# One decoder layer: low parts of the input projection's weights from VectorE to GpSimd, and the values' weights split whole, without precedence

## The chip, the cores and the metric

The kernel runs on one core of one Trainium2 chip. The core has a matrix engine (TensorE, in the profile PE, its weight loads PEld), a vector engine (VectorE, DVE), a scalar engine (ScalarE, ACT), a general one (GpSimd, POOL) and a queue that issues most transfers (SyncE, SP). They have programs of their own and wait for one another by semaphores. The metric is the device time of one execution in microseconds, as the median of three runs.

## The reference

One layer of a hybrid decoder in float32, for 1 x 1024 tokens of 1024 features: a norm, one combined input projection, two mixers on its columns (a gated delta rule with 4 heads of 128, a dilated attention with 8 heads of 64), one output projection, and a gated MLP of 2816 features with a short convolution. Cut to what the change touches:

```python
def hybrid_layer(x, norm1_w, w_in, conv_qkv_w, ...):
    h = rmsnorm(x, norm1_w)
    proj = h @ w_in
    qkv_a, z_a, b_a, a_a, qkv_b = (proj[..., :o1], proj[..., o1:o2], proj[..., o2:o3],
                                   proj[..., o3:o4], proj[..., o4:])
    qkv_a = silu(causal_dwconv(qkv_a, conv_qkv_w))
    qa, ka, va = ...                       # 4 heads of 128 each
    o_a = gated_delta_rule(l2norm(qa) * GDN_HEAD_DIM ** -0.5, l2norm(ka), va, g, beta)
    o_a = rmsnorm(o_a, gdn_norm_w) * silu(z)
    o_b = dilated_attention(qb, kb, vb)    # qb, kb, vb from qkv_b
    x = x + concat(o_a, o_b) @ w_out
    ...                                    # gated MLP, final norm
```

## The kernel before

**Products.** The matrix engine multiplies operands of a shortened float32 format. To keep the precision of float32, each operand is split in a high part (a copy rounded to that format) and a low part (the operand less its high part), and `mm3` makes three products of them: high by high, high by low, low by high. A product is 512 columns wide; the operands' tiles have 128 x 1024 elements.

**Splitting weights.** A raw weight tile `wst` comes by a transfer on SP's queue (`raw_weight`, two buffers). `weight` then writes the high part `whi` on ScalarE (a copy) and the low part `wlo` on VectorE (a subtraction of two tiles in SBUF), two buffers each. With `urgent` it does so in two halves of 512 columns, through `ua` and `uv`, which are ScalarE and VectorE with precedence. `split` is the same without halves and precedence; the operand `x` and others are split by it. So a `wst` buffer is free for the next transfer when both copy and subtraction have read it, and a `whi` or `wlo` buffer when TensorE has made the last product with it.

**Where it happens.** `dense` runs the input projection over a list of columns: the keys' last head, then the values of the dilated attention by token (two groups `V`, eight weight tiles in all, 24 products a tile), then twenty tiles of 48 products each: `q` and `v` of the delta rule's four heads, eight tiles of the attention's queries and keys (`a`), and the four gates `z`. `take` hands out the tile that was prepared, prepares the next one (index `i`), and starts the raw transfer of the one after it. Index 0 is the keys' tile, 1 to 8 are the values', 9 to 28 the twenty others.

`values_by_token` makes four banks of PSUM in a group, over four weight tiles. ScalarE evicts them to `vx`, scaled by the norm `rst`; the second group writes the same four banks and so waits for these evictions.

**What runs beside it.** While the values are projected, the keys' heads are prepared: a convolution of four taps on VectorE (`kT<-xr,gcw,kT`, `xr` being the input), exponentials of the decays on ScalarE (`dec`), transposed keys (`ktok` evictions, sums of squares `sq`), and evictions of the keys' products on VectorE (`um`). Later come the same for queries (`qT`) and values (`vT`), norms on GpSimd (`rq`, a power), a forward substitution in 31 steps on VectorE, clearing of tiles for it on GpSimd (`x`), and then the delta rule's chain and the attention, whose GpSimd work is the copies `rd` and the products `vtok<-vtok,ms`.

**What sets the order.** On TensorE the order is that in which a planner (`Weave`) records the products: `mm` and `tp` stamp each one (L193, L197). On all other engines a scheduler orders the instructions by a priority, which follows the order of recording, and by when it reckons their inputs to be there; instructions made through `ua` and `uv` are put 400 places ahead (L144 in the profile, others L142). GpSimd and VectorE instructions execute in the order fixed thereby.

Of the kernel before, what the change touches and what calls it, by code (L numbers as in the profile page):

```python
# [7 lines left out]
F32 = mybir.dt.float32  # L8
F32R = mybir.dt.float32r
AF = mybir.ActivationFunctionType  # L10
OP = mybir.AluOpType
# [136 lines left out]
def hybrid_layer(tc, I, out):  # L148
    nc = tc.nc
    wv = Weave()  # L150
    ve = Engine(wv, nc.vector, "vector", 0.07, 0.00105)
    ac = Engine(wv, nc.scalar, "scalar", 0.12, 0.00085)

    uv = Engine(wv, nc.vector, "vector", 0.07, 0.00105, first=tc.high_priority)
    ua = Engine(wv, nc.scalar, "scalar", 0.12, 0.00085, first=tc.high_priority)
    po_ = Engine(wv, nc.gpsimd, "gpsimd", 0.15, 0.0021)
# [10 lines left out]
    def tile_(pool, shape, dt, name, tag, bufs):  # L167
        return wv.slot(pool.tile(list(shape), dt, name=name, tag=tag, bufs=bufs), tag, bufs)
# [3 lines left out]
    def A(name, tag, dt=F32, shape=(P, 1024)):  # L172
        if tag in TURNS:
            i = turns[tag] = turns.get(tag, -1) + 1
            tag = TURNS[tag][i % len(TURNS[tag])]
        return tile_(lp, shape, dt, name, tag, SLOTS[tag])
# [23 lines left out]
    def mm3(dst, lhs, rhs, first, last, **kw):  # L200
        us = 0.2135 * rhs[0].shape[-1] / 512
        mm(dst, lhs[0], rhs[0], us, first, False, **kw)
        mm(dst, lhs[0], rhs[1], us, False, False, **kw)
        mm(dst, lhs[1], rhs[0], us, False, last, **kw)

    def split(src, hi, lo):
        ac.activation(hi, src, AF.Copy)
        return ve.tensor_tensor(lo, src, hi.bitcast(F32), op=OP.subtract)

    def raw_weight(src, n=1024):  # L210
        st = tile_(wp, [P, n], F32, "wst", "wst", 2)
        sy.dma_start(st, src)
        return st

    def weight(src, n=1024, st=None, urgent=False):
        if st is None:
            st = raw_weight(src, n)
        hi = tile_(wp, [P, n], F32R, "whi", "whi", 2)
        lo = tile_(wp, [P, n], F32R, "wlo", "wlo", 2)
        for sl in (half(0), half(1)) if urgent else (slice(0, n),):  # L220
            (ua if urgent else ac).activation(hi[:, sl], st[:, sl], AF.Copy)
            (uv if urgent else ve).tensor_tensor(lo[:, sl], st[:, sl], hi[:, sl].bitcast(F32), op=OP.subtract)
        return hi, lo

    def wk_by_halves(src):
# [34 lines left out]
    def bank(tag, name="ps"):  # L260
        return tile_(pp_, (P, 512), F32, name, tag, 2)
# [7 lines left out]
    def half(i):  # L269
        return slice(i * 512, i * 512 + 512)  # L270
# [170 lines left out]
    def scaled(pair, name, by_class=False, tag="ev", t=None, hs=(0, 1)):  # L441
        if t is None:
            t = A(name, tag)
        for h in hs:
            sl = half(h)
            if by_class:
                ve.tensor_tensor(t[:, sl].rearrange("p (n c u) -> p n u c", n=4, c=4),
                                        pair[h].rearrange("p (n u c) -> p n u c", n=4, c=4),
                                        rstdB[:, sl].rearrange("p (n u c) -> p n u c", n=4, c=4), op=OP.mult)
            else:  # L450
                ve.tensor_tensor(t[:, sl], pair[h], rstdB[:, sl], op=OP.mult)
        return t
# [4 lines left out]
    def conv_silu(xr, j, name, tag):  # L457
        y = A(name, tag)
        ac.activation(y, xr, AF.Copy, scale=gcw[:, j, 3:4])
        for d in (1, 2, 3):  # L460
            inst = ve.scalar_tensor_tensor(y[:, d:], xr[:, :S - d], gcw[:, j, 3 - d:4 - d], y[:, d:],
                                           op0=OP.mult, op1=OP.add)
            if j // 4 == 1 and d == 2 and klast:
                after(inst, klast[-1], "the keys before go first")
        if j // 4 != 1:
            ac.activation(y, y, AF.Silu)
            return y

        th = ac.activation(xr, y, AF.Tanh, scale=0.5)
        klast.append(ve.scalar_tensor_tensor(y, xr, 1.0, y, op0=OP.add, op1=OP.mult))  # L470
        kends[j - 4] = th, klast[-1]
        return y

    def silu2(xr, name):
        y = A(name, "ev")
        ac.activation(y, xr, AF.Tanh, scale=0.5)
        ve.scalar_tensor_tensor(y, y, 1.0, xr, op0=OP.add, op1=OP.mult)
        return y
# [8 lines left out]
    def first_keys():  # L487
        xr = [scaled(pst[2 * h:2 * h + 2], "xr", tag=("ev", "ev", "qa")[h]) for h in range(3)]
        for h in range(3):
            T["k", h] = conv_silu(xr[h], 4 + h, "kT", "kT*")  # L490
            wv.add(3, kprep(h))
            yield wv.need(T["k", h])

    def dense():

        yield from wv.until("first")
        yield from wv.until("norms")
        wv.add(2, first_keys())

        srcs, tiles = [], 0  # L500
        for col in DENSE:
            if col[0] == "V":
                srcs += [I["wv"][j] for j in range(4)]
            else:
                srcs.append(I["wi"][tiles])
                tiles += 1
        place = [0]
        raw = [raw_weight(srcs[0])]
        nxt = [weight(None, st=raw.pop())]
        raw.append(raw_weight(srcs[1]))  # L510

        def take():
            w = nxt.pop()
            i = place[0] = place[0] + 1
            if i < len(srcs):
                nxt.append(weight(None, st=raw.pop(), urgent=1 <= i <= 8))
            if i + 1 < len(srcs):
                raw.append(raw_weight(srcs[i + 1]))
            return w

        def values_by_token(g):

            banks = [bank(t) for t in ("asc", "asc", "ch", "ch")]
            for j in range(4):
                w = [t.rearrange("p (k m) -> p k m", k=2) for t in take()]
                for kk in range(2):
                    k = 2 * j + kk
                    for i, pt in enumerate(banks):
                        c = 4 * g + i
                        yield wv.need(pt, *w)  # L530
                        mm3(pt, [t[:, c * P:(c + 1) * P] for t in xs[k]], [t[:, kk, :] for t in w], k == 0, k == KT - 1)
            for i in range(0, 4, 2):
                vx = A("vx", "ev", shape=(P, 2, 512))
                for e in range(2):
                    c = 4 * g + i + e
                    ac.activation(vx[:, e, :], banks[i + e], AF.Copy, scale=rst[:, c:c + 1])
                c = 4 * g + i
                sy.dma_start(vpark[c * P:(c + 2) * P].rearrange("(e p) d -> p e d", e=2), vx)
            wv.done.add(("V", g))

        for i, col in enumerate(DENSE):
            kind, h = col[:2]
            if kind == "V":
                yield from values_by_token(h)
                continue
            if kind == "z":
                yield from wv.until(("o", h))
            w = [t.rearrange("p (k m) -> p k m", k=KT) for t in take()]
            pair = []
            for hh in range(2):  # L550
                pt = bank("hf")
                yield wv.need(pt, *w)
                for k in range(KT):
                    mm3(pt, [t[:, k, :] for t in w], [t[:, half(hh)] for t in xs[k]], k == 0, k == KT - 1)
                    yield 0.0

                pair.append(pt)
                if hh == 0:
                    xr = A("aqkv" if kind == "a" else "xr", "go" if kind == "k" else "ev")
                scaled(pair, "xr", kind == "a", t=xr, hs=(hh,))  # L560
            if kind == "k":
                T["k", h] = conv_silu(xr, 4 + h, "kT", "kT*")
                wv.add(3, kprep(h))
            elif kind == "q":
                q = conv_silu(xr, h, "qT", "qa")
                wv.add(4, qprep(h, q))
            elif kind == "v":
                v = conv_silu(xr, 8 + h, "vT", "qa")
                wv.add(4, vprep(h, v))
            elif kind == "z":  # L570
                og = gated[h] = A("og", "kT*")
                sy.dma_start(og, mixer[h])
                ve.tensor_tensor(og, og, silu2(xr, "zz"), op=OP.mult)
            else:
                sy.dma_start(apark[h, col[2]], xr)
                wv.done.add(col)
        wv.done.add("dense")
# [1067 lines left out]
```

## Time and profile before

| | us |
|---|---|
| median of three runs | 1209.37 (1208.98 to 1209.37) |
| the profiled execution | 1209.18 |
| its span | 1207.4 |
| GpSimd busy | 59.1 |
| ScalarE busy | 576.2 |
| VectorE busy | 925.8 |
| TensorE busy | 1192.3 |

The profile is one execution. A row of the timeline gives the start and the duration in us, the engine, the line, the operation and its tiles (out<-in by the program's names, partitions x elements), and in brackets the engine's idle time just before it with the instruction that ended it; `x3` is a run of three alike, taken together. A row of the waits gives the engine and tile that waited, what released it, the sum, the number of times and the longest. A row of the windows gives each engine's busy time in a stretch, with TensorE's granted clock as a share of full speed. Rows of a tile give the shortest, mean and longest duration in ns and the first and last start.

### The profile page before, as it was taken

How to read it: one execution, taken by the hardware profiler on the slowest of the kernel's cores; microseconds unless marked ns; L12 is line 12 of the kernel's file. 1: busy time of each engine (PE TensorE's matmuls, PEld its weight loads, DVE VectorE, ACT ScalarE, POOL GpSimd, SP SyncE). 2: the span in 40 equal slices, each digit the busy share in tenths (PEclk: the TensorE clock that was granted, in tenths of full speed). 3: DMA queues.
4: the chain of work that ended last, by engine and by line, in shares of the span. 5: the costliest groups of instructions: out<-in, count | busy, mean ns of one | idle time of the engine just before them, and what ended most of it. 6: DMA issues, size and time to landing. Idle time of an engine off the chain costs nothing.

```text
span 1207.4 us, 18350 instructions
## 1 busy us (share of the span) xinstructions
PE 1192.3 (99%) x7068; PEld 986.6 (82%) x7068; DVE 925.8 (77%) x1470; ACT 576.2 (48%) x1134; POOL 59.1 (5%) x78
## 2 busy tenths in 40 slices
PE   9999999999999999999999999999999999999997
PEld 7887888889877778888888888888888888888886
DVE  7683975666466556768988989889898889999865
ACT  7384335356355443655545445444454454444441
POOL 0211010003211000000000000000000000000000
PEclk9999999999999999999999999999999999999999
DMA  7424343435633213544223132231322298556513
GB/s 230 111 75 125 117 120 108 157 102 167 213 118 119 89 36 100 174 136 157 71 69 105 53 105 82 75 105 53 105 65 93 89 366 311 177 163 226 162 57 140
DMA packets 85798, 154.80 MB, mean 128 GB/s; under 512 B 21168, under 2 KB 36304, under 8 KB 85712
## 3 DMA queue, kind: packets, MB, share of 16 engines
q1 hardware_dynamic: 85136, 153.12, 39.3%
q8 instruction: 55, 0.90, 0.3%
q10 hardware_dynamic: 576, 0.52, 0.1%
q14 instruction: 31, 0.25, 0.1%
HBM read 117.68 MB, written 35.93 MB: 127 GB/s over the span
## 4 chain that ended last, share of the span: by engine, by line
PE 93%; DVE 3%; ACT 2%; issue 1%; DMA 1%; SPq 0%; POOLq 0%; POOL 0%; DVEq 0%; ACTq 0%
PE ps L193 44%; PE pa L193 20%; PE dw L193 17%; PE pc L193 10%; PE ps L197 3%; DVE kT L142 1%; DMA xt<-in_xT 1%; DVE wlo L142 0%; ACT dec L142 0%; DVE xr L142 0%; DVE x1h L142 0%; PE pd L193 0%; DVE qT L142 0%; SPq L142 0%; ACT xr L142 0%
## 5 line engine op out<-in xcount | busy, mean ns | idle before, releaser
L193 PE MATMUL dw<-pr 128*128 128x512 f32 (+1 forms) x984 | 211.3, 376 | 0.0
L193 PEld LDWEIGHTS dw<-pr 128*128 128x128 f32 x984 | 176.7, 188 | 33.6
L193 PE MATMUL ps<-xhi,whi 128*128 128x512 f32 x384 | 157.3, 410 | 0.0
L193 PE MATMUL ps<-xlo,whi 128*128 128x512 f32 x384 | 150.0, 391 | 0.8 <-DVE xlo L142 0.8
L193 PE MATMUL ps<-xhi,wlo 128*128 128x512 f32 x384 | 150.2, 391 | 0.0
L193 PE MATMUL pa<-T,pair 128*128 128x512 f32 x528 | 127.0, 389 | 0.0
L193 PEld LDWEIGHTS pa<-T,pair 128*128 128x128 f32 x528 | 99.0, 188 | 20.5
L193 PEld LDWEIGHTS ps<-xhi,whi 128*128 128x128 f32 x384 | 72.2, 188 | 18.1 <-issue 4.7
L193 PEld LDWEIGHTS ps<-xhi,wlo 128*128 128x128 f32 x384 | 72.1, 188 | 15.7 <-DVE wlo L142 0.2
L193 PEld LDWEIGHTS ps<-xlo,whi 128*128 128x128 f32 x384 | 72.4, 188 | 13.4 <-DVE xlo L142 1.1
L142 ACT ACTIVATE u<-pa 128x512 f32<-128x512 f32 x44 | 26.3, 598 | 107.3 <-PE pa L193 107.3
L142 DVE SCALAR_TENSOR_TENSOR y<-xu,fcw,y 128x1023 f32<-128x1023 f32 (+1 forms) x44 | 56.4, 1281 | 22.1 <-ACT y L142 22.0
L142 ACT ACTIVATE whi<-wst 128x1024 fp32r<-128x1024 f32 (+2 forms) x33 | 33.3, 1009 | 68.0 <-PE ps L193 62.4
L193 PE MATMUL pa<-B,A 128*128 128x512 f32 x264 | 63.4, 389 | 0.0
L193 PE MATMUL pc<-T,S 128*128 128x512 f32 x264 | 63.4, 389 | 0.0
L193 PE MATMUL pa<-T,S 128*128 128x512 f32 x264 | 63.4, 389 | 0.0
L193 PE MATMUL pc<-B,pair 128*128 128x512 f32 x264 | 63.4, 389 | 0.0
L142 DVE TENSOR_TENSOR wst<-wst 128x512 f32<-128x512 f32 x88 | 60.4, 687 | 0.9
L193 PE MATMUL ps<-B,pair 128*128 128x512 f32 x252 | 60.5, 389 | 0.0
L144 ACT ACTIVATE sm<-sm,mx 128x128 f32<-128x128 f32 (+7 forms) x64 | 35.4, 556 | 50.5 <-DVE mx L144 50.5
L193 PEld LDWEIGHTS pa<-T,S 128*128 128x128 f32 x264 | 49.6, 188 | 10.3
L193 PEld LDWEIGHTS pc<-T,S 128*128 128x128 f32 x264 | 49.6, 188 | 10.3
(245 smaller groups left out, 2344.7 us busy)
## 6 DMA issues: line engine op xcount, KB each, us to landing
wst<-in_wu SPq DMA_DIRECT2D x44, 512.0 KB, 3.7
wd<-in_wd SPq DMA_DIRECT2D x44, 512.0 KB, 4.5
upark<-y SPq DMA_DIRECT2D x22, 512.0 KB, 3.7
wst<-in_wi SPq DMA_DIRECT2D x21, 512.0 KB, 3.7
r<-upark SPq DMA_DIRECT2D x11, 512.0 KB, 7.5
r<-upark SPq DMA_DIRECT2D x22, 256.0 KB, 6.8
wa<-in_wd SPq DMA_DIRECT2D x22, 256.0 KB, 3.1
wst<-in_wv SPq DMA_DIRECT2D x8, 512.0 KB, 3.7
```

The lines of the kernel that those rows point to most:

```text
L142: return getattr(eng, op)(*a, **kw)
L144: return getattr(eng, op)(*a, **kw)
L193: tc.stamp_issue_order_token(nc.tensor.matmul(dst, lhs, rhs, start=start, stop=stop, **kw).ins, TOKEN)
L197: tc.stamp_issue_order_token(nc.tensor.transpose(dst, src, ident if idt is None else idt).ins, TOKEN)
```

## The change

The halves and the precedence go out of `weight`. For indices 9 to 28 (the twenty tiles from the first query head onwards) the high part is copied by ScalarE as before, and the low part is subtracted by GpSimd (`po_`) instead of VectorE. For the values' eight tiles the split is whole, on ScalarE and VectorE, without precedence; the keys' tile stays as it was.

```diff
-    def weight(src, n=1024, st=None, urgent=False):
+    def weight(src, n=1024, st=None, spare=False):
         if st is None:
             st = raw_weight(src, n)
         hi = tile_(wp, [P, n], F32R, "whi", "whi", 2)
         lo = tile_(wp, [P, n], F32R, "wlo", "wlo", 2)
-        for sl in (half(0), half(1)) if urgent else (slice(0, n),):
-            (ua if urgent else ac).activation(hi[:, sl], st[:, sl], AF.Copy)
-            (uv if urgent else ve).tensor_tensor(lo[:, sl], st[:, sl], hi[:, sl].bitcast(F32), op=OP.subtract)
+        if spare:
+            ac.activation(hi, st, AF.Copy)
+            po_.tensor_tensor(lo, st, hi.bitcast(F32), op=OP.subtract)
+        else:
+            split(st, hi, lo)
         return hi, lo
...
             if i < len(srcs):
-                nxt.append(weight(None, st=raw.pop(), urgent=1 <= i <= 8))
+                nxt.append(weight(None, st=raw.pop(), spare=i >= 9))
```

The order of TensorE's products changes by a few places only. On the other engines it moves at these places. (The rows of the order call `TENSOR_SCALAR` what the profile's rows call `SCALAR_TENSOR_TENSOR`, an operation with two tiles and a scalar.)

ScalarE, from the middle of the first group of values to its last eviction; before:

```order
L144 ACTIVATE whi<-wst 128x512 x2
L142 ACTIVATE xr<-kT 128x1024
L142 ACTIVATE dec<-dec,ngc 128x128 x8
L142 ACTIVATE ge<-gel 128x8
L144 ACTIVATE whi<-wst 128x512 x2
```

and after that, at its evictions:

```order
L142 ACTIVATE vx<-ps,rst 128x512 x3
L142 ACTIVATE dec<-dec,ngc 128x128 x5
L144 ACTIVATE whi<-wst 128x512 x2
L142 ACTIVATE dec<-dec,ngc 128x128 x3
L142 ACTIVATE eg<-gend 128x8
L142 ACTIVATE ge<-gel 128x8
L142 ACTIVATE vx<-ps,rst 128x512
```

The same two pieces in the changed kernel, in one:

```order
L142 ACTIVATE xr<-kT 128x1024
L142 ACTIVATE whi<-wst 128x1024
L142 ACTIVATE dec<-dec,ngc 128x128 x8
L142 ACTIVATE ge<-gel 128x8
L142 ACTIVATE whi<-wst 128x1024
...
L142 ACTIVATE vx<-ps,rst 128x512 x2
L142 ACTIVATE dec<-dec,ngc 128x128 x8
L142 ACTIVATE eg<-gend 128x8
L142 ACTIVATE ge<-gel 128x8
L142 ACTIVATE vx<-ps,rst 128x512 x2
L142 ACTIVATE whi<-wst 128x1024
```

`xr` goes ahead of the copy `whi`. Two evictions `vx` instead of one stand behind the eight `dec`, and the copy of the next tile stands behind them all.

VectorE, at the fourth and fifth of the values' tiles; before:

```order
L142 TENSOR_SCALAR kT<-xr,gcw,kT 128x1021
L144 TENSOR_TENSOR wlo<-wst,whi 128x512 x2
L142 TENSOR_SCALAR ssk<-ssk 128x8
L142 RECIPROCAL bp<-ssk 128x8
L142 TENSOR_TENSOR bp<-bp,beta 128x8
L144 TENSOR_TENSOR wlo<-wst,whi 128x512
L142 TENSOR_TENSOR ke<-bp,eg 128x8
L142 TENSOR_SCALAR um<-ps,bp,dec 128x128
L144 TENSOR_TENSOR wlo<-wst,whi 128x512
L142 TENSOR_SCALAR um<-ps,bp,dec 128x128 x3
L142 TENSOR_SCALAR kT<-xr,kT 128x1024
L142 COPY gel<-dec 128x8
```

and in the changed kernel:

```order
L142 TENSOR_SCALAR kT<-xr,gcw,kT 128x1021
L142 TENSOR_TENSOR wlo<-wst,whi 128x1024
L142 TENSOR_SCALAR ssk<-ssk 128x8
L142 RECIPROCAL bp<-ssk 128x8
L142 TENSOR_TENSOR bp<-bp,beta 128x8
L142 TENSOR_TENSOR ke<-bp,eg 128x8
L142 TENSOR_SCALAR kT<-xr,kT 128x1024
L142 COPY gel<-dec 128x8
L142 TENSOR_SCALAR kT<-xr,gcw,kT 128x1022
L142 TENSOR_SCALAR um<-ps,bp,dec 128x128 x4
L142 TENSOR_TENSOR wlo<-wst,whi 128x1024
```

The fourth tile's low part keeps its place as one instruction; the fifth's moves behind the next head's convolution products and four evictions `um`.

GpSimd, from the first query head onwards; before:

```order
L142 MEMSET xi 128x1024
L142 AFFINE_SELECT xi<-xi 128x1024
L142 TENSOR_TENSOR rq<-ssq,mhalf 128x8
L142 MEMSET x_1672 128x1024
L142 MEMSET x_1686 128x1024
L142 TENSOR_TENSOR rq<-ssq,mhalf 128x8 x3
```

and in the changed kernel:

```order
L142 MEMSET xi 128x1024
L142 AFFINE_SELECT xi<-xi 128x1024
L142 TENSOR_TENSOR wlo<-wst,whi 128x1024 x4
L142 TENSOR_TENSOR rq<-ssq,mhalf 128x8
L142 TENSOR_TENSOR wlo<-wst,whi 128x1024
L142 MEMSET x_1653 128x1024
L142 MEMSET x_1667 128x1024
L142 TENSOR_TENSOR wlo<-wst,whi 128x1024
L142 TENSOR_TENSOR rq<-ssq,mhalf 128x8
```

The low parts stand between the norms `rq` and the clearing of `x`; the other fourteen follow among the later work of GpSimd.

## The prediction, made before the changed kernel had been run

> **What bounds the kernel now.** I read the page first, then the waits of TensorE, then the windows and the timeline of the two places which the waits name.
>
> ```profile
> span 1207.4 us, 18350 instructions
> PE 1192.3 (99%) x7068; PEld 986.6 (82%) x7068; DVE 925.8 (77%) x1470; ACT 576.2 (48%) x1134; POOL 59.1 (5%) x78
> PE 93%; DVE 3%; ACT 2%; issue 1%; DMA 1%; SPq 0%; POOLq 0%; POOL 0%; DVEq 0%; ACTq 0%
> ```
>
> TensorE works for 1192.3 of 1207.4 us, and it makes up 93% of the chain that ended last. So 15.1 us at most can be won from waits, and an edit that takes VectorE off work wins only where TensorE waits for VectorE. These are TensorE's waits that lie at the instructions of the change:
>
> ```profile
> PE ps L193 <- ACT vx L142: 2.1, 1, 2.1
> PE ps L193 <- DVE wlo L144: 1.1, 1, 1.1
> ```
>
> Each is one single wait. The windows say how full the stages are in which the changed instructions run (values by token in the first, then heads):
>
> ```profile
> core 0: us, PE busy (x) PEld busy (x) DVE busy (x) ACT busy (x) POOL busy (x), PEclk, DMA share, GB/s
> 40.00:100.00 60.00, 56.79 (x276) 46.54 (x274) 42.62 (x78) 40.34 (x131) 10.98 (x7) 0.97 0.38 101
> 100.00:150.00 50.00, 50.00 (x246) 42.23 (x245) 36.77 (x84) 17.43 (x42) 5.51 (x4) 1.00 0.37 112
> 200.00:250.00 50.00, 49.79 (x551) 41.41 (x551) 28.21 (x52) 20.80 (x56) 3.22 (x2) 1.00 0.38 127
> ```
>
> From 40 to 100 us TensorE lacks 3.2 us; from 100 to 150 it lacks none, and from 200 to 250 only 0.2. The first half of the change works where there is something to win, the second where there is nearly nothing. The first window has a second oddity, a clock of 0.97, and a finer cut finds its place:
>
> ```profile
> 92.00:96.00 4.00, 1.89 (x10) 1.24 (x9) 1.29 (x2) 2.83 (x9) 0.00 (x0) 1.00 0.61 100
> 96.00:99.50 3.50, 3.50 (x14) 2.81 (x12) 0.00 (x0) 1.63 (x9) 0.00 (x0) 0.51 0.77 265
> ```
>
> Directly behind the emptiest stretch (1.89 of 4 us busy) the granted clock is 0.51 for 3.5 us. At half speed these 3.5 us hold work for 3.5 x 0.51 = 1.8 us, so the clock costs 1.7 us beside the wait.
>
> **The change, part one: the eight tiles of the values.** It removes the halving and the precedence; nothing else is taken out or added. By size alone it saves: two half subtractions become one whole, and the same for the copies.
>
> ```profile
> L142 DVE TENSOR_TENSOR wlo<-wst,whi x23: 1202/1225/1425, 29.9 to 476.9; 128x1024 fp32r<-128x1024 f32 x23
> L144 DVE TENSOR_TENSOR wlo<-wst,whi x18: 679/684/694, 32.0 to 498.9; 128x512 fp32r<-128x512 f32 x18
> ```
>
> A whole low part takes 1.22 us and two halves 2 x 0.684 = 1.37, 0.15 us more. What matters is when TensorE gets them. At the fourth value tile (the first wait) it is this:
>
> ```profile
> 73.54 0.50 PE L193 MATMUL ps<-whi,xhi 128*128 128x512 f32 x1
> 75.15 0.50 PE L193 MATMUL ps<-wlo,xhi 128*128 128x512 f32 x1 [1.11 <-DVE wlo L144]
> 70.57 3.92 DVE L142 SCALAR_TENSOR_TENSOR kT<-xr,gcw,kT 128x1023 f32<-128x1023 f32 x3 [0.23 <-ACT kT L142]
> 74.41 1.29 DVE L144 TENSOR_TENSOR wlo<-wst,whi 128x512 fp32r<-128x512 f32 x2
> ```
>
> The three convolution passes fill VectorE up to 74.4 in both versions, since its order there stays. The first half was ready at 74.41 + 0.68 = 75.1, and TensorE went on at 75.15. The whole tile is ready at 74.4 + 1.22 = 75.6: this wait grows by **0.46 us**. Copying the high part whole costs nothing, because VectorE is the later of the two.
>
> The next tile loses its precedence on VectorE, and is put behind one convolution product and four evictions of `um`:
>
> ```profile
> 82.57 0.39 PE L193 MATMUL ps<-wlo,xhi 128*128 128x512 f32 x1
> 76.92 1.24 ACT L144 ACTIVATE whi<-wst 128x512 fp32r<-128x512 f32 x2
> 77.96 1.15 ACT L142 ACTIVATE xr<-kT 128x1024 f32<-128x1024 f32 x1
> 80.01 1.21 DVE L142 SCALAR_TENSOR_TENSOR kT<-xr,kT 128x1024 f32<-128x1024 f32 x1
> 82.41 1.12 DVE L142 SCALAR_TENSOR_TENSOR um<-ps,bp,dec 128x128 f32<-128x128 f32 x4
> ```
>
> ScalarE now does `xr` before `whi`, so `xr` ends at about 76.9 + 1.1 = 78.0 and the product behind it starts then, 2 us before its old place. From its start to the end of the four evictions were 83.53 - 80.01 = 3.5 us; by that the low part runs from 81.5 to 82.7. TensorE wants it at 82.57 + 0.46 = 83.0. I cost this at nothing, with 0.3 us of cover; without that cover, each tenth more is a tenth on the span.
>
> The second wait is ScalarE's. Four banks must be evicted (`vx`) before the second group of values can write them:
>
> ```profile
> 81.33 2.46 ACT L142 ACTIVATE dec<-dec,ngc 128x128 f32<-128x128 f32 x8 [2.23 <-DVE gel L142]
> 83.80 1.14 ACT L144 ACTIVATE whi<-wst 128x512 fp32r<-128x512 f32 x2
> 88.83 1.88 ACT L142 ACTIVATE vx<-ps,rst 128x512 f32<-128x512 f32 x3
> 92.00 1.19 ACT L144 ACTIVATE whi<-wst 128x512 fp32r<-128x512 f32 x2
> 94.12 0.71 ACT L142 ACTIVATE vx<-ps,rst 128x512 f32<-128x512 f32 x1
> 91.92 0.40 PE L193 MATMUL ps<-whi,xhi 128*128 128x512 f32 x1
> 94.89 0.50 PE L193 MATMUL ps<-whi,xhi 128*128 128x512 f32 x1 [2.11 <-ACT vx L142]
> ```
>
> Three evictions ran at 88.83; the fourth stood behind the eight `dec` and behind the two urgent halves of 92.00, and TensorE waited 2.1 us for its bank. In the new order two evictions run first, then `dec`, two small ones, then two evictions, and the copy of the next tile only after them. ScalarE also arrives earlier: `dec` at 81.33 had waited 2.2 us for VectorE, whose product came 2 us later than it will. So the copy at 83.80 starts as soon as TensorE has left its buffer, near 83.0, and the row behind it moves up by about 0.75 us. By durations: first two evictions 88.1 to 89.35 (1.88 / 3 = 0.63 each), eight `dec` 2.46 to 91.8, the small ones to 92.1, the last two to 93.35. TensorE comes to the third bank at 91.92 + 0.46 = 92.4 and waits there until 92.8, and the fourth bank's products start near 93.5, not 94.89: **1.4 us earlier**, with the 0.46 already paid (so -1.86 for the wait itself). Bounds: nothing if `dec` is late again, -1.65 (2.11 less 0.46) if no wait remains.
>
> The **clock**: the only stretch at half speed follows a gap of over 2 us, and the gap of 1.1 us ahead of 75.15 was followed by none. With gaps of 0.4 us left here, I take the half clock as gone: **-1.7 us**; the other bound is 0. [...]
>
> **Part two: twenty low parts go to GpSimd.** VectorE is relieved of 20 x 1.22 = 24.5 us. GpSimd has no such subtraction in this trace; the nearest row is its own two-input operation of the same size:
>
> ```profile
> 288.60 1.90 POOL L142 TENSOR_TENSOR vtok<-vtok,ms 128x1024 f32<-128x1024 f32 x1
> 289.96 0.56 DVE L142 TENSOR_SCALAR ms<-ms 128x8 f32<-128x8 f32 x1 [0.28 <-ACT osq L144]
> 312.59 0.17 DVE L142 TENSOR_SCALAR ms<-ms 128x8 f32<-128x8 f32 x1 [0.47 <-ACT osq L144]
> ```
>
> So 1.9 us a tile, 38 us on an engine that was busy 59. The two rows beside it show a cost to VectorE: a tiny operation of 0.17 us lasts 0.56 when it meets GpSimd's, and both end at 290.5. [...]
>
> ```profile
> wst<-in_wi SPq DMA_DIRECT2D x21, 512.0 KB, 3.7
> 115.62 1.06 ACT L142 ACTIVATE whi<-wst 128x1024 fp32r<-128x1024 f32 x1 [6.10 <-PE ps L193]
> 121.31 0.39 PE L193 MATMUL ps<-xhi,wlo 128*128 128x512 f32 x1
> ```
>
> For the first query tile the high part is there at 116.7 and the low part wanted at 121.3, 4.6 us of cover. For an upper bound on GpSimd I add one VectorE pass that it waits out (1.3 us, a third of the 3.92 above): 3.2 us, still covered; less than 1.9 has no row for it. Later tiles are prepared a whole tile ahead, 48 products of 50.00 / 246 = 0.2 us, near 10 us. The raw tile is released some 0.7 to 2 us later, and its successor's load on SP's queue lands in 3.7 us, inside those 10. GpSimd's own queue holds short work behind the subtractions (`rq`, `rd` copies), which is then late by up to 1.9 us; I cost that at nothing, for TensorE's full windows show no place that leans on it, and at 1.9 us each if one did. One place has no cover at all, the fourth query head:
>
> ```profile
> 215.02 1.22 DVE L142 TENSOR_TENSOR wlo<-wst,whi 128x1024 fp32r<-128x1024 f32 x1 [0.18 <-ACT whi L142]
> 216.16 1.28 DVE L142 SCALAR_TENSOR_TENSOR qT<-xr,gcw,qT 128x1023 f32<-128x1023 f32 x1
> 222.31 0.77 PE L197 MATMUL ps<-ident,qT 128*128 128x128 f32 x5 [0.21 <-ACT qT L142]
> ```
>
> There TensorE already waits 0.2 us at the end of the `qT` passes. If the pass at 216.16 has to sit out GpSimd's subtraction, it begins at 216.9 instead: +0.7; if GpSimd gives way, it begins up to 1.2 us earlier and the 0.2 us go. Between -0.2 and +0.7 I take +0.2, and the same net nothing for the other 19.
>
> **Sum:** +0.46 - 1.86 - 1.7 + 0.2 = -2.9 us. The profiled execution took 1209.18 us (its span of 1207.4 and 1.8 around it), which is 0.2 under the median of the runs, 1209.37. 1209.18 - 2.9 = **1206.3 us**.
>
> **Rivals.**
>
> First, the half clock stays or moves: the gap at the fourth tile grows from 1.1 to about 1.6 us, nearer the 2.1 which was followed by half clock. Then only 1.2 us are won: 1208.0. For it: I have just these two gaps to set the limit from. Against: 1.6 is still below 2.1. [...]
>
> Second, the wait for `vx` stays: `dec` is held up by VectorE as at 81.33, and the two evictions that are now behind all eight of them come as late as the one did. Then +0.46 and +0.2, with the clock as before: 1209.8. Against it: the product ahead of `dec` moves up by 2 us.
>
> Third, slower: GpSimd and VectorE shut each other out, and each low part costs VectorE 1.9 - 1.22 = 0.68 us more than it gave. Over 20 tiles that is 13.6 us. It decides once it reaches TensorE in more than five tiles (3.1 / 0.68 = 4.6 uses up the gain); at 10 of 20 it is +6.8 - 3.1, **1212.9 us**. For it: the `ms` pair, and the convolutions, which read two tiles each and start all through the heads. Against: VectorE is busy 28.2 of 50 us at the heads from 200 to 250, so 0.68 us have room, and TensorE's wait there is 0.2 us in total.
>
> **How the numbers follow.** The forecast gets 0.43, the first rival 0.25, the second 0.12, the third 0.20. What a measurement of this kernel can tell from no change is about 0.2%, 2.4 us: faster means under 1207.0, slower over 1211.8. The forecast varies by the 0.3 us of cover, the bounds of the wait and GpSimd's ±0.5, so 1205 to 1208: four fifths of it are faster, 0.35, the rest same. The first rival spreads from 1206.5 to 1209, 0.08 faster and 0.17 same. The second is same, 0.01 to slower. The third is slower in 0.18 and same in 0.02. Together 0.43 faster, 0.38 same, 0.19 slower. The range goes from 1204.4 (all gains at their bounds, -1.65 - 1.7 - 0.2, and one subtraction of 1.22 where VectorE's relief might reach TensorE once more) to 1211.8, leaving out most of the third rival and little below; the forecast's own range is 1205 to 1208.
>
> **What would show it.** In the waits, `vx` falls from 2.1 to under 0.6 and `wlo` rises from 1.1 to about 1.6. The windows show clock 1.00 from 72 to 103; a 0.5 behind the fourth tile speaks for the first rival. GpSimd's busy time goes to about 97 us, its `wlo` group reads near 1.9 us, and VectorE's falls by about 26. At the fourth query head the wait for `qT` lies between 0 and 0.9. The prediction is wrong if TensorE's busy time grows, if waits on `wlo` of GpSimd appear, or if VectorE's passes beside them lengthen and TensorE waits for them in the heads.

## The result, and the profile after

| | median us | lowest to highest | runs |
|---|---|---|---|
| before | 1208.70 | 1206.42 to 1210.53 | 20 |
| changed | 1206.57 | 1205.53 to 1208.53 | 20 |

The ratio is 0.9983, 95% interval 0.9977 to 0.9989: the change wins about 2.1 us, 0.17%. The profiled execution took 1205.66 us with a span of 1203.8. One correction of names: the text ahead of this section counts from the keys' tile, so that what it calls the fourth and fifth value tile are the third and fourth of the values. Tiles are counted here from the first of the values.

The page and TensorE's waits of the changed kernel (columns as before):

```profile
span 1203.8 us, 18327 instructions
PE 1190.0 (99%) x7068; PEld 984.8 (82%) x7068; DVE 917.5 (76%) x1442; ACT 575.1 (48%) x1126; POOL 108.9 (9%) x98
PE ps L197 <- DVE at L142: 1.5, 1, 1.5
PE ps L193 <- DVE wlo L142: 0.9, 1, 0.9
```

The wait on `vx` is gone and a new one stands at the top: 1.5 us on VectorE's `at` (evictions of the products of keys and queries in the delta rule's heads), in a stage where TensorE never waited. GpSimd is busy 49.8 us more. VectorE is busy only 8.3 us less, though subtractions of 24.5 us were taken off it. The windows show where time was won and lost:

```profile
40.00:100.00 60.00, 59.07 (x298) 48.92 (x297) 44.17 (x82) 42.45 (x135) 14.52 (x9) 1.00 0.38 102
100.00:150.00 50.00, 49.71 (x243) 41.41 (x242) 37.97 (x78) 14.72 (x30) 12.50 (x7) 1.00 0.38 111
150.00:200.00 50.00, 48.37 (x342) 39.85 (x341) 33.56 (x55) 22.90 (x65) 17.14 (x9) 1.00 0.46 127
92.00:96.00 4.00, 4.00 (x23) 3.30 (x23) 1.23 (x1) 3.15 (x12) 0.00 (x0) 1.00 0.59 164
96.00:99.50 3.50, 3.50 (x21) 3.03 (x20) 1.92 (x6) 2.27 (x10) 1.82 (x2) 1.00 0.64 155
```

From 40 to 100 us TensorE is busy 59.07 instead of 56.79, at clock 1.00 instead of 0.97. From 92 to 96 it is full where it had 1.89 of 4, and no half clock follows. But from 150 to 200 it now lacks 1.6 us, where it lacked nothing before:

```profile
150.00:200.00 50.00, 50.00 (x354) 41.79 (x353) 35.57 (x64) 22.27 (x64) 5.62 (x4) 1.00 0.45 127
```

ScalarE's timeline at the evictions, with TensorE's third bank, has the order that the prediction laid out, and runs 0.8 to 1.1 us sooner than reckoned there:

```profile
87.27 1.34 ACT L142 ACTIVATE vx<-ps,rst 128x512 f32<-128x512 f32 x2
88.41 2.51 ACT L142 ACTIVATE dec<-dec,ngc 128x128 f32<-128x128 f32 x8
90.95 1.32 ACT L142 ACTIVATE vx<-ps,rst 128x512 f32<-128x512 f32 x2
91.75 0.50 PE L193 MATMUL ps<-whi,xhi 128*128 128x512 f32 x1
```

All four evictions end at 92.27 instead of 94.83, and TensorE passes with hardly a stop.

GpSimd's low parts, all twenty in one row of the groups, then the one of `v1` with the step of VectorE that met it, the next step of that kind, and the wait of TensorE twelve us on (timelines of the three engines):

```profile
L142 POOL TENSOR_TENSOR wlo<-wst,whi 128x1024 fp32r<-128x1024 f32 x20 | 47.7, 2385 | 123.0 <-ACT whi L142 121.3 <-PE ps L197 1.8
141.64 2.42 POOL L142 TENSOR_TENSOR wlo<-wst,whi 128x1024 fp32r<-128x1024 f32 x1 [10.36 <-ACT whi L142]
142.26 2.04 DVE L142 TENSOR_TENSOR xi<-xi,tmp 128x220 f32<-128x220 f32 x1
144.75 0.38 DVE L142 TENSOR_TENSOR xi<-xi,tmp 128x207 f32<-128x207 f32 x1
154.05 0.66 PE L197 MATMUL ps<-ident,vT 128*128 128x128 f32 x4 [1.47 <-DVE at L142]
```

A low part takes GpSimd 2.39 us, not the 1.9 that I read from `vtok`. A step of the forward substitution lasts 2.04 us where the next one, a little smaller, takes 0.38; it ends 0.24 us after GpSimd's instruction. In the chain that ended last, the stretch from 105 to 150 us has turned from TensorE (one piece of 44 us before) to VectorE, with two more long steps in it, each beside a low part of GpSimd. TensorE's wait stands at the end of this chain:

```profile
118.84 2.49 DVE xi L142
129.07 2.51 DVE xi L142
```

```profile
99.93 44.21 PE ps L193 x211
```

(The first of these fences is the changed kernel's chain, the second that of before; start, duration, what.)

### The profile page after: what moved, and what is told of

It is laid out like the page before. It is cut to its first block, busy times and chain, and to the rows that moved or that the text cites. A ratio compares the mean times of both kernels' runs of the same rounds, so it can differ in the third digit from the quotient of the medians.

```text
span 1203.8 us, 18327 instructions
## 1 busy us (share of the span) xinstructions
PE 1190.0 (99%) x7068; PEld 984.8 (82%) x7068; DVE 917.5 (76%) x1442; ACT 575.1 (48%) x1126; POOL 108.9 (9%) x98
## 4 chain that ended last, share of the span: by engine, by line
PE 90%; DVE 6%; ACT 2%; issue 1%; DMA 1%; SPq 0%; POOLq 0%; POOL 0%; DVEq 0%; ACTq 0%
PE ps L193 40%; PE pa L193 20%; PE dw L193 17%; PE pc L193 10%; PE ps L197 2%; DVE xi L142 1%; DVE kT L142 1%; DVE tmp L142 1%; DVE xr L142 1%; DMA xt<-in_xT 1%; ACT sm L144 0%; DVE qT L142 0%; DVE vT L142 0%; SPq L142 0%; DMA mt<-mdram 0%
## 5 line engine op out<-in xcount | busy, mean ns | idle before, releaser
L142 ACT ACTIVATE whi<-wst 128x1024 fp32r<-128x1024 f32 (+2 forms) x41 | 41.9, 1021 | 76.2 <-PE ps L193 48.0
L142 POOL TENSOR_TENSOR rs<-rs,mhalf 128x2 f32<-128x2 f32 (+2 forms) x4 | 4.5, 1116 | 738.8 <-DVE rs L144 738.8
L142 POOL TENSOR_TENSOR wlo<-wst,whi 128x1024 fp32r<-128x1024 f32 x20 | 47.7, 2385 | 123.0 <-ACT whi L142 121.3
```

The source lines that it names most:

```text
L142: return getattr(eng, op)(*a, **kw)
```

## The experiments

The table has every run. Each ratio is to runs of the kernel before made beside it, of which some have the half clock and some not (below); each kernel ran 5, 11 or 20 times. The lead is how much earlier (minus) or later TensorE starts its first product with a weight tile than in the profile of before, from the matmul rows of the timelines: at the sixth value tile (100.9 us in before), at `v1` (157.1), `v3` (213.9), in the attention (384.7), and behind the input projection (498.3). The profile of before had the half clock, which makes 1.6 us of each lead. Up to 0.3 us more or less in a lead arose ahead of the value stage.

| kernel | ratio to before | 95% interval | lead at 100.9 | 157.1 | 213.9 | 384.7 | 498.3 |
|---|---|---|---|---|---|---|---|
| the change | 0.9983 | 0.9977 to 0.9989 | -4.0 | -1.2 | -1.2 | -4.4 | -3.9 |
| values only | 0.9977 | 0.9969 to 0.9986 | -3.5 | -3.5 | -3.4 | -3.4 | -3.4 |
| GpSimd only | 1.0017 | 1.0008 to 1.0026 | -1.8 | +1.6 | +1.6 | -1.6 | -1.1 |
| vx first | 0.9977 | 0.9969 to 0.9986 | -4.7 | -4.7 | -4.7 | -4.7 | -4.7 |
| before again | 0.9994 | 0.9985 to 1.0003 | -0.1 | 0.0 | 0.0 | -0.1 | -0.1 |
| GpSimd from q2 | 0.9955 | 0.9942 to 0.9967 | -3.3 | -3.3 | -3.2 | -6.3 | -5.9 |
| GpSimd for the first four | 1.0010 | 1.0001 to 1.0018 | -3.6 | -0.2 | -0.2 | -0.3 | -0.3 |
| order put back | 0.9989 | 0.9980 to 0.9997 | -4.1 | -0.8 | -0.7 | -3.9 | -3.4 |
| vx first, GpSimd from q2 | 0.9955 | 0.9941 to 0.9968 | -3.7 | -3.7 | -3.7 | -6.8 | -6.3 |
| planned only | 0.9956 | 0.9944 to 0.9969 | -3.3 | -3.3 | -3.3 | -4.9 | -4.3 |
| executed only | 0.9950 | 0.9937 to 0.9964 | -3.6 | -3.6 | -3.6 | -5.7 | -6.0 |
| first four twice | 0.9983 | 0.9975 to 0.9992 | -3.3 | +1.1 | +1.1 | -2.0 | -1.5 |
| first four in eighths | 0.9963 | 0.9949 to 0.9976 | -1.9 | -1.2 | -1.1 | -4.3 | -3.8 |

### The two halves apart, the evictions alone, and before once more

The edits named GpSimd only, vx first, and vx first with GpSimd from q2 are made to the kernel before; where they use `spare`, `weight` also gets the branch `if spare` of the change, which is not printed again. All other edits are made to the changed kernel. The run before again has no edit.

```diff
-                nxt.append(weight(None, st=raw.pop(), spare=i >= 9))
+                nxt.append(weight(None, st=raw.pop(), spare=False))
```

> Only the values' half of the change: their eight tiles are split whole without precedence, and all twenty later low parts stay on VectorE. Theory (the gain is made in the value stage, by the wait on vx and the half clock behind it; GpSimd's share adds about nothing): ratio to the kernel before 0.9975 to 0.9990, the clock 1.00 from 72 to 103 us, the wait on vx gone. Rival 1 (the gain is made by VectorE's relief): ratio 0.999 to 1.001 although the value stage looks as in the changed kernel. Rival 2 (GpSimd's share costs time): ratio below 0.997, faster than the whole change.

```diff
-                nxt.append(weight(None, st=raw.pop(), urgent=1 <= i <= 8))
+                nxt.append(weight(None, st=raw.pop(), urgent=1 <= i <= 8, spare=i >= 9))
```

> Only GpSimd's half: twenty low parts on GpSimd, the values' tiles in urgent halves as before. Theory: ratio 0.999 to 1.001, the wait on vx of 2.1 us and the half clock are still there, and VectorE's passes with two SBUF inputs that meet a low part on GpSimd last up to 2.4 us longer. Rival 1: ratio 0.9975 to 0.999, as in the whole change. Rival 2: ratio above 1.001.

```diff
-                    ac.activation(vx[:, e, :], banks[i + e], AF.Copy, scale=rst[:, c:c + 1])
+                    ua.activation(vx[:, e, :], banks[i + e], AF.Copy, scale=rst[:, c:c + 1])
```

> The kernel before with one thing changed: the evictions vx have precedence on ScalarE, so that the fourth runs ahead of the urgent halves of the next tile; everything else, the halves too, as before. Theory (the wait on vx and the clock behind it are the gain): the wait on vx falls below 1 us, no half clock follows, ratio 0.997 to 0.999. Rival (the clock falls for another reason): the wait falls but some 3.4 us at half clock remain in the value stage, ratio 0.9985 to 1.000.

> The kernel before, profiled once more. If the half clock follows from the gap of 2.1 us alone, it is there again, at the same place, for some 3.5 us. [...] Ratio 0.999 to 1.001.

The values' half wins 0.23% alone, GpSimd's loses 0.17% alone. That GpSimd's share adds nothing is not borne out by the run with GpSimd only, whose interval lies wholly above 1. The threshold set for the rival that it costs time (the values alone below 0.997) was not reached either. Multiplied, the two halves would give 0.9994; the change has 0.9983, and the intervals, taken together, are too wide to say whether the halves simply add. Giving `vx` precedence, one letter in the kernel before, wins the same 0.9977 as the values' half: moving the fourth eviction is enough, and neither whole tiles nor their lower precedence are needed for it. (In its profile the lead is larger, -4.7, by 0.8 us won at the third value tile; the section on the prediction says from what.)

The clock came out differently from what I had thought. The windows of the kernel before taken again, then of the kernel with GpSimd only, whose value stage is that of before, gap and all:

```profile
92.00:96.00 4.00, 1.91 (x7) 1.19 (x6) 1.29 (x2) 2.77 (x9) 0.00 (x0) 0.87 0.63 94
96.00:99.50 3.50, 3.50 (x16) 2.90 (x15) 0.00 (x0) 1.63 (x9) 0.00 (x0) 0.66 0.74 267
```

```profile
92.00:96.00 4.00, 1.91 (x11) 1.30 (x10) 1.29 (x2) 2.62 (x8) 0.00 (x0) 1.00 0.62 88
96.00:99.50 3.50, 3.50 (x19) 2.88 (x18) 0.00 (x0) 3.18 (x19) 0.00 (x0) 1.00 0.72 260
```

In the second kernel's window nothing is slowed. In the first, the half clock lies 1.1 us earlier than in the first profile of before (there 0.50 from 96.1 to 99.5 us), and so falls in both rows; cut to it, the row reads:

```profile
95.00:98.40 3.40, 3.40 (x11) 2.73 (x12) 0.00 (x0) 1.17 (x7) 0.00 (x0) 0.50 0.87 258
```

The same wait of 2.1 us was followed by half clock in two executions and by none in the third. So its cost is paid in some executions only. The mean granted clock that each run recorded bears this out. A half clock of 3.4 us takes 3.4 x 0.50 / 1208 = 0.0014 off that mean. The end of an execution has a slower clock too (0.64 over the last 7.4 us of before, so that the stretch at 96 us is not the only slow one there; 0.58 over the last 8.8 of the changed kernel), and the eleven profiles that have clock 1.00 from 20 to 150 us stand at 0.997 or 0.998. Of the 78 runs of before beside the experiments, 41 are at 0.996 or below and take 1209.5 us in the mean, ten are at 0.998 and take 1207.5; the others, at 0.997, can be either. Of the changed kernel's 20 runs, two are at 0.996 (1208.3 us), the others above (1206.3). Of the 22 runs of the values' half and of `vx` first, none is at 0.996. Where in those runs the half clock lay is not shown.

### Which of GpSimd's twenty, and is it the order?

```diff
-                nxt.append(weight(None, st=raw.pop(), spare=i >= 9))
+                nxt.append(weight(None, st=raw.pop(), spare=i >= 13))
```

> The changed kernel, but the first four of the twenty low parts (q0, v0, q1, v1, those that are made while VectorE runs the forward substitution) go back to VectorE; sixteen stay on GpSimd. Theory (the changed kernel loses 2.8 us on the way through these four tiles and nothing behind them): no loss at 140 to 157 us, ratio 0.9955 to 0.9975. If the 2.7 us that the changed kernel gained from 213 to 498 us come from VectorE's relief there, they stay: ratio near 0.9955. Rival (that gain is only the loss caught up): ratio 0.997 to 0.9985, as with the values' half alone.

```diff
-                nxt.append(weight(None, st=raw.pop(), spare=i >= 9))
+                nxt.append(weight(None, st=raw.pop(), spare=9 <= i <= 12))
```

> The counterpart: only the low parts of q0, v0, q1 and v1 on GpSimd, the sixteen later ones on VectorE, the values' half as in the changed kernel. Theory (these four carry the loss): the loss of some 2.8 us at 140 to 157 us is there, ratio 0.999 to 1.0005. Rival (it is caught up downstream whatever the later tiles do): ratio 0.9975 to 0.9985.

```diff
                 scaled(pair, "xr", kind == "a", t=xr, hs=(hh,))
+                if kind in "qv" and h < 2 and (kind, h) != ("v", 1):
+                    n = {"q0": (10, 15), "v0": (17, 20), "q1": (22, 28)}[kind + str(h)][hh]
+                    after(steps[n], evicted[-1], "the eviction goes first")
```

(`steps` collects the substitution's products, `evicted` the evictions `xr`.)

> The changed kernel with VectorE's order put back: dependencies on the same engine hold the forward substitution's steps 10, 15, 17, 20, 22 and 28 behind the evictions xr of q0, v0 and q1, where they stood before; all twenty low parts stay on GpSimd. If the scheduler's pulling of two or three more steps ahead of these evictions is the cause of the loss, it goes: ratio 0.9955 to 0.9975. If it is that GpSimd's low part shuts VectorE out (a step of 0.4 us lasting 2.0 to 2.5), the loss stays: ratio 0.998 to 0.999, as in the changed kernel.

With four of the twenty back on VectorE, 0.9983 becomes 0.9955; with those four alone on GpSimd it becomes 1.0010. So the four cost (0.9983 - 0.9955) x 1209 = 3.4 us, and the other sixteen win (0.9977 - 0.9955) x 1209 = 2.7 us, each to some 1.8 us by the intervals. The change's small net is a difference of two larger terms. The order is not it: with the six evictions of `q0`, `v0` and `q1` back in their old places the lead still falls from -4.1 to -0.8, and the step behind an eviction is as long as in the changed kernel, or longer (VectorE's timeline of the kernel with the order put back):

```profile
141.03 0.68 DVE L142 TENSOR_TENSOR xr<-ps,rstdB 128x512 f32<-128x512 f32 x1
141.63 2.43 DVE L142 TENSOR_TENSOR tmp<-mt,xi 128x231 f32<-128x231 f32 x1
```

### Is it the exclusion?

```diff
...
             split(st, hi, lo)
+            if twice:
+                nc.gpsimd.tensor_tensor(lo, st, hi.bitcast(F32), op=OP.subtract)
...
-                nxt.append(weight(None, st=raw.pop(), spare=i >= 9))
+                nxt.append(weight(None, st=raw.pop(), spare=i >= 13, twice=9 <= i <= 12))
```

> As the run with GpSimd from q2 onwards, but the low parts of q0, v0, q1 and v1, which VectorE subtracts there, are subtracted by GpSimd once more into the same tiles; the orders of VectorE and TensorE are the same as in that run, to the last instruction. So GpSimd's four instructions are added and nothing is taken off VectorE. If GpSimd's subtraction shuts VectorE out: three or four steps of the forward substitution last 2 to 2.5 us instead of 0.3 to 0.4, VectorE is late by 6 to 8 us, and the run takes 3 to 8 us more than that one, ratio 0.998 to 1.002. If it does not: ratio 0.9945 to 0.9965.

```diff
...
-            po_.tensor_tensor(lo, st, hi.bitcast(F32), op=OP.subtract)
+            wv.account("gpsimd", 0.15 + 0.0021 * n, [lo], [st, hi], 0.28)
+            for j in range(pieces):
+                sl = slice(j * n // pieces, (j + 1) * n // pieces)
+                nc.gpsimd.tensor_tensor(lo[:, sl], st[:, sl], hi[:, sl].bitcast(F32), op=OP.subtract)
...
-                nxt.append(weight(None, st=raw.pop(), spare=i >= 9))
+                nxt.append(weight(None, st=raw.pop(), spare=i >= 9, pieces=8 if i <= 12 else 1))
```

> The changed kernel, but GpSimd subtracts the first four low parts (q0, v0, q1, v1) in eight pieces of 128 columns; the planner books the same time as before, and the orders of TensorE, VectorE and ScalarE are those of the changed kernel to the last instruction. If GpSimd keeps VectorE out for the length of one instruction and lets it in between two, steps of the forward substitution last some 0.6 to 0.8 us instead of 2.0 to 2.5, several in a row, and part of the 2.8 us lost at 140 to 157 us comes back: ratio 0.996 to 0.998. If VectorE is kept out until all pieces are done, or pays for each the same: one step still lasts 2 us or more, ratio 0.998 to 0.9995.

Four instructions are added on an idle engine, none taken off VectorE, no order of VectorE or ScalarE changed: 0.9955 becomes 0.9983, 3.4 us, and the lead falls by 4.4 us at the same place. TensorE doesn't wait for the second writing of the low parts: the waits that are new in this kernel are for what VectorE and, behind it, ScalarE deliver.

```profile
PE ps L197 <- ACT qT L142: 1.9, 1, 1.9
PE ps L197 <- DVE at L142: 1.3, 1, 1.3
```

So the loss is that of VectorE being kept out while GpSimd's subtraction runs, called the exclusion from here on. In VectorE's timeline of the kernel that does them twice, a step takes 2.44 us, and two convolution passes 3.42 where 1.28 is usual:

```profile
122.30 2.44 DVE L142 TENSOR_TENSOR tmp<-mt,xi 128x192 f32<-128x192 f32 x1
133.61 3.42 DVE L142 SCALAR_TENSOR_TENSOR qT<-xr,gcw,qT 128x1023 f32<-128x1023 f32 x1
145.55 3.42 DVE L142 SCALAR_TENSOR_TENSOR vT<-xr,gcw,vT 128x1023 f32<-128x1023 f32 x1
```

In eighths the engines take turns. GpSimd's row and three of VectorE's of that kernel:

```profile
142.09 5.02 POOL L225 TENSOR_TENSOR wlo<-wst,whi 128x128 fp32r<-128x128 f32 x8 [4.93 <-ACT whi L142]
142.71 0.51 DVE L142 TENSOR_TENSOR xi<-xi,tmp 128x220 f32<-128x220 f32 x1
143.25 0.52 DVE L142 TENSOR_TENSOR tmp<-mt,xi 128x207 f32<-128x207 f32 x1
143.81 0.52 DVE L142 TENSOR_TENSOR xi<-xi,tmp 128x207 f32<-128x207 f32 x1
```

A step lasts 0.52 instead of 2.04, this low part of GpSimd 5.0 us instead of 2.4, which the cover allows, and the ratio is 0.9963 with VectorE's and ScalarE's orders those of the changed kernel. So VectorE is kept out for one instruction at a time. This profile's lead of -1.9 at 100.9 has a cause of its own, another half clock, behind the waits at the third value tile (0.5 us for `whi` and 1.1 for `wlo`):

```profile
72.00:76.00 4.00, 2.40 (x10) 1.46 (x9) 3.27 (x3) 4.00 (x19) 0.00 (x0) 1.00 0.00 0
76.00:80.00 4.00, 4.00 (x16) 3.52 (x15) 3.03 (x7) 3.57 (x12) 1.64 (x1) 0.57 0.48 131
```

### Where the other sixteen win

Moving low parts changes two things: what VectorE does, and TensorE's order, since the planner books VectorE less. Each was tried without the other, for the sixteen from `q2` onwards. `pv` is VectorE booked as GpSimd, `vp` GpSimd booked as VectorE:

```diff
+    pv = Engine(wv, nc.vector, "gpsimd", 0.15, 0.0021)
...
-            po_.tensor_tensor(lo, st, hi.bitcast(F32), op=OP.subtract)
+            pv.tensor_tensor(lo, st, hi.bitcast(F32), op=OP.subtract)
```

> As the run with GpSimd from q2 onwards, but the sixteen low parts are executed by VectorE while the planner books them on GpSimd. TensorE's order is that of the run with GpSimd from q2, to the last product; the work is distributed as in the values' half alone. If the later gain (2.4 us between 213 and 498 us) comes from TensorE's order, which the planner changes by a few groups because it books VectorE less, it stays: ratio 0.9945 to 0.9965. If it comes from VectorE doing less, it goes: ratio 0.997 to 0.9985.

```diff
+    vp = Engine(wv, nc.gpsimd, "vector", 0.07, 0.00105)
...
-            po_.tensor_tensor(lo, st, hi.bitcast(F32), op=OP.subtract)
+            vp.tensor_tensor(lo, st, hi.bitcast(F32), op=OP.subtract)
```

> The counterpart: the sixteen low parts are executed by GpSimd while the planner books them on VectorE, so that TensorE's order is that of the values' half alone, to the last product. If the later gain comes from VectorE doing less: ratio 0.9945 to 0.9965. If it comes from TensorE's order: ratio 0.997 to 0.9985.

Both ratios (0.9956 and 0.9950) reach that of the two together, so neither either-or holds: each half of the move gains by itself, and the ratios can't share the gain out. The traces give a hint, each in one execution: from 100.9 to 498.3 us the order alone gains 1.0 us, the relief alone 2.4, both 2.6; they don't add. One place where the relief works is in the attention. The timelines of the values' half alone, then of GpSimd executing what VectorE is booked for:

```profile
349.03 1.21 DVE L142 TENSOR_TENSOR wlo<-wst,whi 128x1024 fp32r<-128x1024 f32 x1
350.50 0.46 DVE L144 COPY pb<-ps 128x128 f32<-128x128 f32 x2
351.01 1.42 PE L193 MATMUL ps<-kT,qT 64*128 64x128 f32 x6 [0.17 <-DVE pb L144]
```

```profile
349.38 0.45 DVE L144 COPY pb<-ps 128x128 f32<-128x128 f32 x2
350.38 0.94 PE L194 MATMUL ps<-kT,qT 64*128 64x128 f32 x8
```

There a low part stood ahead of the copies `pb`, and TensorE's eight products of scores came in starts and stops, 1.1 us later at the end; without it they run through. The copies read PSUM, and a GpSimd subtraction running at the same time (349.0 to 351.4) doesn't touch them: 0.45 us for two, where it is 0.46 without it. The kernel with GpSimd executing also shows what the fourth query head costs where the planner doesn't help, in TensorE's waits:

```profile
PE ps L198 <- ACT qT L142: 1.3, 1, 1.3
```

### A version better than both

```diff
-                nxt.append(weight(None, st=raw.pop(), urgent=1 <= i <= 8))
+                nxt.append(weight(None, st=raw.pop(), urgent=1 <= i <= 8, spare=i >= 13))
...
-                    ac.activation(vx[:, e, :], banks[i + e], AF.Copy, scale=rst[:, c:c + 1])
+                    ua.activation(vx[:, e, :], banks[i + e], AF.Copy, scale=rst[:, c:c + 1])
```

> A candidate for a version better than both: the kernel before with the evictions vx given precedence, the values' urgent halves kept, and the low parts from q2 onwards on GpSimd. If both gains add: ratio 0.994 to 0.9965. If GpSimd's share adds nothing there: ratio 0.997 to 0.9985, as with the evictions alone.

The kernel before with `vx` first and GpSimd from `q2` onwards takes 1203.25 us, 0.9955 of before, as does the changed kernel with the four given back (1203.57). Each of the two is faster than the kernel before and than the changed one.

## Why the prediction was right, and where it was not

**The value stage: right.** The waits and clock were to give +0.46 - 1.86 - 1.7 = -3.1 us; the values' half alone measured 0.9977, -2.8 us, and led by 3.5 us in its profile, 0.2 of them from ahead of the value stage. Term by term:

- The wait on `vx` fell from 2.1 us to none in the list, by the order of evictions that was reckoned. Right; the values' half alone gains 2.1 us here, somewhat more than the 1.86.
- The half clock is gone in the profile of the changed kernel. Right for the executions compared, but wrong as a rule: a gap of 2.1 us was followed by it twice and once not, and gaps of 1.6 us in all (the kernel in eighths) once. So the 1.7 us are not won in each run: by their mean clocks, an estimate, at least 41 of 78 runs of before paid them and at least ten did not. The first rival, that the half clock moves to the tile ahead, came true in the one profiled execution of the kernel in eighths (0.57 from 76 to 80 us). What makes the same gap be followed by half clock in one execution and not in another, no run shows.
- The wait for the whole low part, +0.46: the values' half alone has TensorE busy 2.50 of 4 us from 72 to 76, against 2.89 before, 0.39 more idle; its lead behind that place changes by 0.44. Right; it stands in the waits as 1.1 for `wlo` and 0.4 for `whi`. In the profile of the change itself the wait was only 0.9, and that is luck. VectorE's passes began at 69.77 instead of 70.57, because four earlier passes had taken 6.76 us instead of 7.59 (VectorE's timelines of before, then of the change):

```profile
51.74 7.59 DVE L142 SCALAR_TENSOR_TENSOR kT<-xr,gcw,kT 128x1023 f32<-128x1023 f32 x4
```

```profile
51.86 6.76 DVE L142 SCALAR_TENSOR_TENSOR kT<-xr,gcw,kT 128x1023 f32<-128x1023 f32 x4
```

  Beside these passes GpSimd works on four tiles `dec`. A pass takes 1.28 us undisturbed; beside GpSimd three of the four last 2.1 in before, two in the change. Of the fourteen profiles eleven have three such passes (VectorE is busy 15.1 to 15.4 us from 40 to 60 us) and three have two (14.8), and the change's own order stands on both sides. So VectorE was already being kept out in the kernel before.

**GpSimd's share: the net about right, the terms wrong.** The prediction put +0.2 at the fourth query head and "the same net nothing for the other 19". Against the values' half alone the measured net is (0.9983 - 0.9977) x 1209 = +0.7 us, within the intervals of nothing. But the step that failed is that "net nothing": four of the tiles cost 3.4 us and sixteen win 2.7. That the two nearly cancel is luck: with the first four alone on GpSimd the ratio is 1.0010, no gain at all. By the prediction's own list of what would show it wrong, one sign came: VectorE's instructions beside the low parts lengthen, and TensorE waits for them in the heads (1.5 us on `at`). VectorE's busy time, too, fell by 8.3 us and not by 26.

The cover of each low part, reckoned as TensorE's wait for `wlo`, was never touched, as said; what was missed is who else is on VectorE, and whether TensorE waits at its end. During the first four its work is a chain of dependent steps with two sources in SBUF, and TensorE waits behind it. Three of them met GpSimd's subtraction and lost 1.7 to 2.2 us each, while the subtractions taken away had cost 1.2 each; the first of the four had lain in idle time ahead of the substitution and gave nothing. From `q2` on, eight of the sixteen met a convolution pass or a product with two sources in SBUF and lengthened it, by 0.7 to 1.3 us, as this one of `v2` (timelines of GpSimd and VectorE of the changed kernel; undisturbed the pass takes 1.28):

```profile
168.00 2.39 POOL L142 TENSOR_TENSOR wlo<-wst,whi 128x1024 fp32r<-128x1024 f32 x1 [6.52 <-ACT whi L142]
168.99 2.48 DVE L142 SCALAR_TENSOR_TENSOR vT<-xr,gcw,vT 128x1023 f32<-128x1023 f32 x1 [1.27 <-ACT vT L142]
```

That is 8.6 us in all, against 16 x 1.22 = 19.5 us of subtractions taken away, and no wait of 0.2 us or more on such a pass stands in TensorE's list. Copies and evictions from PSUM kept their durations beside GpSimd (`xr` 0.68 us, `pt` of 256 columns 0.40 to 0.42, `wke` 0.34 to 0.35).

**The size of GpSimd's subtraction** was taken as 1.9 us from `vtok`, whose second source is a small tile; it is 2.39, 1.95 times VectorE's 1.22.

**The fourth query head** was costed at +0.2 between -0.2 and +0.7. In the changed kernel the wait is below 0.2, since the planner put the transposes of `qT` six products later; with the old order it is 1.3 instead of 0.2, +1.1 where the bound was +0.7. That GpSimd's subtraction is 0.5 us longer than reckoned accounts for the difference.

**The rivals.** The third, that GpSimd and VectorE shut each other out, was right in its mechanism and wrong in its size and place. It put 0.68 us on each of twenty. Measured, VectorE lost 0.4 to 0.9 us more than it was given on each of three, within 0.6 us of what it was given on eight more, and nothing on the other nine; TensorE waited for the three. GpSimd's half without the values' did make the kernel slower (1.0017). The second, that `vx` stays, did not occur.

## What to carry to other kernels

A subtraction of two full tiles given to GpSimd left VectorE's copies and evictions from PSUM untouched here (`xr` 0.68 us, `pt` 0.40 to 0.42), but kept out, until its end, each VectorE instruction with two sources in SBUF that came while it ran: eleven in the changed kernel, which took 0.7 to 2.2 us longer. (One source in SBUF is no sure escape: in the prediction's rows a tiny `ms<-ms` beside GpSimd's product takes 0.56 us instead of 0.17.) So give GpSimd the tiles whose time falls on evictions, or on passes for which nothing waits; keep it from a chain of two-source steps at whose end TensorE waits, or cut it into short pieces. When one engine waits for a bank, look for what stands ahead of the eviction in its queue: giving that one eviction precedence did as much here as reworking eight tiles. A small net of a change in several parts is worth taking apart: here 0.17% hid 0.45%. And moving work between engines in the planner's books alone, with the work left where it was, changes TensorE's order: that gained 1.0 us by the trace of one execution.

## What the hardware showed that was not expected

- The exclusion is per instruction: a step of 0.2 to 0.4 us lasts 2.04 to 2.5 beside one instruction of GpSimd of 2.4 us, and 0.46 to 0.53 beside eight pieces that take 4.2 us together (`v0` in the kernel in eighths).
- It works both ways: in the kernel in eighths, GpSimd's eight pieces take 3.4 us at `q0`, most of them while VectorE is idle, 4.2 at `v0` beside steps alone, and 6.1 at `q1` and 5.0 at `v1`, where convolution passes run as well.
- The half clock behind a gap is not decided by the gap alone: 2.1 us of waiting were followed by half clock for 3.4 us in two executions (0.50 in both profiles of before) and by none in a third (1.00 with GpSimd only).
